# One decoder trunk on one Trainium2 core: transposes of x and single x convolutions stated one behind each weight piece, and the last group's sums stated later

## The chip, the cores and the metric

The kernel runs on one core of one Trainium2 chip. The metric is device time in microseconds (us), one launch; the time before is 1239.31 us, the median of 3 runs (1236.56 to 1241.85). A core has TensorE (PE, matmuls; its weight loads are listed as PEld), VectorE (DVE), ScalarE (ACT), GpSimd (POOL) and SyncE (SP, which here issues DMAs). Each engine works its own queue in order, and waits on semaphores for what others produce.

## The reference, cut to what matters

Two layers over 256 tokens of width 2048. The change lies in layer 0, a Mamba-2 (SSD) mixer with 8 groups of 8 heads:

```python
proj = h @ in_w                                   # z, x, B, C, dt
xBC = silu(conv4(xBC) + b)                        # causal, depthwise, 4 taps
dt = softplus(dt + dt_bias); A = -exp(A_log)
acum = cumsum(dt * A)                             # one chunk of 256 tokens
decay = exp(where(causal, acum_l - acum_s, -inf))
y = einsum("blsgk,bsgkp->blgkp", (C . B) * decay, x * dt)
y = (y + x * D_skip) * silu(z)
yg = y * rsqrt(mean(y ** 2, per group of 512) + eps)
out = (yg * norm_g) @ out_w
```

Layer 1 (dilated attention) and the two layer norms stay as they are.

## The kernel before, in words

All weights are streamed once. A weight arrives in **pieces** of 512 KB (`raw`, 6 buffers, DMAs issued by SP). ACT rounds a piece to `whi` (L100), DVE takes the rest as `wlo = raw - whi` (L102), and PE multiplies with both halves. There are 4 buffers of each half, so the split of a piece waits until PE is done with the piece four before it. A piece of `cm_quad` is 24 matmuls (L151, L152 with `whi`, L153 with `wlo`); a piece of `cm_wide` (L194, L197) is 16 matmuls; a piece of the output product is 12 (L228). In the text the pieces are numbered in the order of their splits from the kernel's start, P70, P151 and so on, with whi#151 and wlo#151 as their halves.

The SSD stage is a loop over groups g. An iteration states, in this order: the product of B and C for the next two groups (odd g only), `scores(g)` (C times B, two matmuls L739, L740), the product of x of group g+1, `stage3` of group g-1, `stage1(g)`, the four convolutions of x of group g+1 (`convolve`), the product of z of group g+1 and `stage2(g)`.

- A convolution `conv` is an ACT scaling (L389), three DVE multiply-adds (L392) and an ACT silu (L394).
- `stage1` takes the decays: relu (L757, 16 times) and exp (L759, twice, and L761, 4 times) on ACT, a DVE product (L762), then 8 transposes of x on PE (L770) with three DVE products out of PSUM (L772 `xd` twice, L777 `xo`), and four ACT copies (L781).
- `stage2`: matmuls L791 and L802, DVE L793, L794, L805, L806, an ACT square (L808). `stage3`: DVE sums L813, L815 and the small matmuls L818, then L820 and a reciprocal root.

Silu and exp/relu lie in different tables of ACT, so that an `ACT_TABLE_LOAD` stands wherever the queue goes from one kind to the other.

The order within each engine is fixed when the program is built: by a scheduler that takes instructions by the place of their statement and their priority (`tc.high_priority()` draws a block forward, `tc.issue_after` puts an instruction behind a named one). `background` states pieces of other work (the adaLN product on DVE, L320) between weight pieces. `latest[-1]` is the last stated split's DVE instruction. After the loop a product runs (`last_scores` at its third piece, q == 2, states stage3 of group 6 and scores and stage1 of group 7), then stage2 of group 7, then `out_pieces`, the output product over the normed groups, to which `y_ahead(q)` is called at each piece; `ylo` (L879) are the low halves of the normed y that it multiplies.

## Time and profile before

| | |
|---|---|
| median of 3 runs | 1239.31 us (1236.56 to 1241.85) |
| the profiled execution, time | 1240.34 us |
| the profiled execution, span | 1238.5 us |
| mean granted TensorE clock | 0.994 |
| SSD stage in the span | about 200 to 533 us |
| HBM read | 332.50 MB, 271 GB/s over the span |

The span is the profiled part of one execution; the time beside it includes what lies around it (1.84 us). Of a row of the timeline, the first number is the start in us from the span's start, the second how long the group on that row was busy, and in brackets stands how long the engine was idle before it and what released it. In a wait table the numbers are total us, times, longest. PEclk is the granted clock of TensorE as a share of full speed.

### The profile page before, as it was taken

The numbers are of one execution on the slowest core, as the hardware profiler recorded it, in microseconds if no ns is written. First come the engines' busy times: TensorE is split into PE (matmuls) and PEld (weight loads), VectorE is DVE, ScalarE is ACT, GpSimd is POOL, SyncE is SP. The second block draws the span as 40 slices with busy tenths as digits, with TensorE's granted clock in tenths as the row PEclk, the third lists the DMA queues.
The fourth block names the chain that finished last, engine by engine and source line by source line (L and its number), as shares of the span: only waits on it lengthen the run. The fifth ranks groups of instructions, "written<-read, shape, count | busy, mean of one in ns | idle before, by whom it ended". The sixth has DMA issues, their size and how long they took to land.

```text
span 1238.5 us, 20144 instructions
## 1 busy us (share of the span) xinstructions
PE 1210.6 (98%) x7772; PEld 1074.9 (87%) x7772; DVE 1026.3 (83%) x1450; ACT 711.5 (57%) x1056; POOL 12.5 (1%) x21
## 2 busy tenths in 40 slices
PE   8999999899999999979999999999999999999998
PEld 8999999888999998868888888888888888888886
DVE  6999987899888999999788678788996885756886
ACT  4555467787698899644344365443444844444751
POOL 0000000000000000000000000000000000000001
PEclk9999999999999999989999999999999999999999
DMA  9999976785767658689898668989997785355563
GB/s 374 421 421 422 422 273 232 250 312 162 217 227 200 153 204 209 145 255 358 324 370 337 244 221 320 352 347 361 373 392 283 276 269 175 115 188 170 189 257 68
DMA packets 81969, 337.06 MB, mean 272 GB/s; under 512 B 9537, under 2 KB 10321, under 8 KB 69073
## 3 DMA queue, kind: packets, MB, share of 16 engines
q1 hardware_dynamic: 80496, 333.59, 75.3%
q0 software_dynamic: 1168, 2.11, 1.0%
q8 instruction: 61, 1.00, 0.3%
q14 instruction: 36, 0.29, 0.1%
q10 hardware_dynamic: 208, 0.08, 0.0%
HBM read 332.50 MB, written 3.24 MB: 271 GB/s over the span
## 4 chain that ended last, share of the span: by engine, by line
PE 73%; DVE 11%; ACT 7%; DMA 6%; issue 3%; SPq 0%; DVEq 0%; ACTq 0%
PE acc L228 23%; PE acc L194 21%; PE acc L197 11%; DMA raw<-in_win 3%; DVE wlo L102 3%; DVE araw L320 3%; PE acc L153 3%; PE acc L151 3%; PE acc L152 3%; ACT whi L100 2%; DVE cacc L392 2%; DMA araw<-in_ada 2%; ACT seg L757 1%; PE py L802 1%; PE acc L238 1%
## 5 line engine op out<-in xcount | busy, mean ns | idle before, releaser
L100 ACT ACTIVATE whi<-raw 128x1024 fp32r<-128x1024 f32 x389 | 408.1, 1057 | 345.0 <-PE acc L194 105.7
L102 DVE TENSOR_TENSOR wlo<-raw,whi 128x1024 fp32r<-128x1024 f32 x389 | 470.2, 1221 | 135.9 <-ACT whi L100 130.5
L194 PE MATMUL acc<-actT,whi 128*128 128x512 f32 x1280 | 401.4, 394 | 0.0
L197 PEld LDWEIGHTS acc<-actT,wlo 128*128 128x128 f32 x1280 | 239.5, 188 | 54.5 <-DVE wlo L102 2.3
L197 PE MATMUL acc<-actT,wlo 128*128 128x256 f32 x1280 | 254.8, 280 | 1.5 <-DVE wlo L102 1.3
L153 PE MATMUL acc<-actT,wlo 128*128 128x256 f32 x884 | 242.1, 279 | 7.9 <-DVE wlo L102 7.9
L151 PE MATMUL acc<-actT,whi 128*128 128x256 f32 x884 | 245.4, 280 | 1.3 <-ACT whi L100 0.7
L152 PE MATMUL acc<-actT,whi 128*128 128x256 f32 x884 | 244.6, 278 | 0.0
L320 DVE SCALAR_TENSOR_TENSOR araw<-araw,cb__72 128x2048 f32<-128x2048 f32 x95 | 217.1, 2285 | 2.0 <-DMA araw<-in_ada 1.7
L194 PEld LDWEIGHTS acc<-actT,whi 128*128 128x128 f32 x1280 | 194.8, 188 | 0.6
L153 PEld LDWEIGHTS acc<-actT,wlo 128*128 128x128 f32 x884 | 164.8, 189 | 10.1 <-DVE wlo L102 9.9
L151 PEld LDWEIGHTS acc<-actT,whi 128*128 128x128 f32 x884 | 166.9, 189 | 2.9 <-ACT whi L100 0.9
L152 PEld LDWEIGHTS acc<-actT,whi 128*128 128x128 f32 x884 | 166.9, 189 | 0.2 <-issue 0.2
L228 PE MATMUL acc<-whi,actT 128*128 128x512 f32 x560 | 144.4, 392 | 0.5 <-ACT whi L100 0.5
L228 PEld LDWEIGHTS acc<-whi,actT 128*128 128x128 f32 x560 | 105.1, 189 | 23.0 <-ACT whi L100 0.9
L228 PE MATMUL acc<-wlo,actT 128*128 128x512 f32 x384 | 104.1, 393 | 0.0
L228 PEld LDWEIGHTS acc<-wlo,actT 128*128 128x128 f32 x384 | 72.7, 189 | 16.0
L228 PE MATMUL acc<-whi,ylo 128*128 128x512 f32 x208 | 57.4, 399 | 1.4 <-DVE ylo L879 1.4
L228 PEld LDWEIGHTS acc<-whi,ylo 128*128 128x128 f32 x208 | 39.7, 191 | 10.1 <-DVE ylo L879 1.5
L757 ACT ACTIVATE seg<-cbc,cumT 128x128 f32<-128x128 f32 x128 | 40.9, 388 | 5.1 <-PE py L802 3.4
L392 DVE SCALAR_TENSOR_TENSOR cacc<-xs,prm,cacc 128x255 f32<-128x255 f32 (+2 forms) x84 | 37.4, 478 | 2.4 <-ACT cacc L389 2.1
L524 ACT ACTIVATE htmp<-xt,mod 128x256 f32<-128x256 f32 x16 | 9.6, 600 | 31.0 <-DVE mod L325 29.3
(331 smaller groups left out, 1092.6 us busy)
## 6 DMA issues: line engine op xcount, KB each, us to landing
araw<-in_ada SPq DMA_DIRECT2D x96, 1024.0 KB, 7.5
raw<-in_win SPq DMA_DIRECT2D x109, 512.0 KB, 9.4
raw<-in_wout SPq DMA_DIRECT2D x64, 512.0 KB, 7.2
raw<-in_wbin SPq DMA_DIRECT2D x64, 512.0 KB, 4.0
raw<-in_wxs SPq DMA_DIRECT2D x48, 512.0 KB, 4.7
raw<-in_wv SPq DMA_DIRECT2D x48, 512.0 KB, 7.2
raw<-in_wk SPq DMA_DIRECT2D x48, 512.0 KB, 7.7
cbc<-cumd SPq DMA_DIRECT2D x16, 512.0 KB, 6.2
```

What stands on the lines that cost most here:

```text
L100: copied.append(S.activation(hi, raw, AF.Copy))
L102: latest.append(V.tensor_tensor(lo, raw, hi.bitcast(F32), op=ALU.subtract))
L151: T.matmul(o, hi[:, k, c_], ahi[:, kt, :], start=first, stop=False, skip_group_check=True)
L152: T.matmul(o, hi[:, k, c_], alo[:, kt, :], start=False, stop=False, skip_group_check=True)
L153: end = T.matmul(o, lo[:, k, c_], ahi[:, kt, :], start=False, stop=kt == k1 - 1, skip_group_check=True)
L194: T.matmul(ps[n], hi[:, k, n * P:n * P + P], both(kt), start=kt == 0, stop=False, skip_group_check=True)
L197: T.matmul(ps[n][:, 0, :], lo[:, k, n * P:n * P + P], high(kt), start=False, stop=kt == KT - 1, skip_group_check=True)
L228: T.matmul(ps[b], a_(kt)[:, b * P:b * P + P], w_[:, k, :], start=a_ is ahi and w_ is hi and kt == k0, stop=w_ is lo and kt == k1 - 1)
L238: end = T.matmul(o, l_, hi[:, k, :], start=False, stop=kt == k1 - 1, skip_group_check=part)
L320: return V.scalar_tensor_tensor(raw, raw, 1.0, cb_, op0=ALU.mult, op1=ALU.mult, accum_out=mod[layer][:, ct, j:j + 1])
L392: V.scalar_tensor_tensor(acc[:, o:], ps[:, :L - o], w[:, j:j + 1], acc[:, o:], op0=ALU.mult, op1=ALU.add)
L757: S.activation(seg[:, hh, b, :], cbc[:, hh, b, :], AF.Relu, bias=cumT[:, b, h0 + hh:h0 + hh + 1], scale=-1.0)
```

## The change

`stage1` is cut in two. What remains makes the decays and the four ACT copies; the new `by_tokens` makes the transposes with `xd` and `xo`, and its DVE instructions are put behind the latest `wlo`. `xs_conv` and `xs_wide` return four single convolutions, each with its DVE part behind the latest `wlo`. These become entries of a list `chores`: first `unit` (stage3 of the group before and `by_tokens`), then the four convolutions; `cm_quad` takes one entry behind a piece from its second on, `cm_wide` likewise. What is left of an older list is emptied ahead of stage1, and `unit` at the latest ahead of stage2. `stage3` of the last group is stated at q == 8 of the first output chunk, without high priority, where it was at q == 1 with it, and the last group's `y_tiles` at q == 6 of the second chunk, where it was at q == 2.

```diff
@@ -174,6 +174,8 @@
                 begin_next()
             end = cm_piece(src, q, ps, ahi, alo, k0=k0, w=w)
             background(*rate)
+            if chores and q > k0 // 2:
+                chores.pop(0)()
         z_end[:] = [end]
         return ps
 
@@ -197,6 +199,8 @@
                     T.matmul(ps[n][:, 0, :], lo[:, k, n * P:n * P + P], high(kt), start=False, stop=kt == KT - 1,
                              skip_group_check=True)
             background(*rate)
+            if chores and q > 0:
+                chores.pop(0)()
         def put():
             for n in range(2):
                 d = dst[:, n, :]
@@ -382,15 +386,16 @@
                      ("bc", 6): (win[3], 12, y[5]), ("z", 6): (win[12], 12, y[6]), ("z", 5): (win[11], 10, y[7])}
             xs, bc, sz = {}, {}, dict(enumerate(szt))
 
-            def conv(ps, ct, dst):
+            def conv(ps, ct, dst, after=None):
 
                 w = pv("convw")[:, 4 * ct:4 * ct + 4]
                 acc = p0.tile([P, L], F32, name="cacc", bufs=3)
                 S.activation(acc, ps, AF.Identity, bias=pv("convb")[:, ct:ct + 1], scale=w[:, 3:4])
                 for j in (2, 1, 0):
                     o = 3 - j
-                    V.scalar_tensor_tensor(acc[:, o:], ps[:, :L - o], w[:, j:j + 1], acc[:, o:],
-                                           op0=ALU.mult, op1=ALU.add)
+                    with tc.issue_after(after) if after is not None else ExitStack():
+                        V.scalar_tensor_tensor(acc[:, o:], ps[:, :L - o], w[:, j:j + 1], acc[:, o:],
+                                               op0=ALU.mult, op1=ALU.add)
                 S.activation(dst, acc, AF.Silu)
 
             def bc_conv(g, t):
@@ -401,8 +406,7 @@
 
             def xs_conv(g, t):
                 xs[g] = xst[g]
-                for i in range(4):
-                    conv(t[i], 4 * g + i, xs[g][:, i, :])
+                return [lambda i=i: conv(t[i], 4 * g + i, xs[g][:, i, :], latest[-1].ins) for i in range(4)]
 
             def hh_(kt):
                 return hhi[:, kt, :]
@@ -414,11 +418,7 @@
                     cm_wide(wxs[2 * g - 4 + w], t[:, 2 * w:2 * w + 2, :], rate=R,
                             moving=(lambda kt: hp[:, :, kt, :], hh_))
 
-                def convolve():
-                    for n in range(4):
-                        conv(t[:, n, :], 4 * g + n, t[:, n, :])
-
-                return convolve
+                return [lambda n=n: conv(t[:, n, :], 4 * g + n, t[:, n, :], latest[-1].ins) for n in range(4)]
 
             def product(kind, g, pre=None):
 
@@ -447,7 +447,7 @@
                                             op=ALU.add)
                     t = [part[:, n, :] for n in range(4)]
                 if kind == "xs":
-                    return lambda: xs_conv(g, t)
+                    return xs_conv(g, t)
                 bc_conv(g, t)
 
             with ExitStack() as c0:
@@ -695,7 +695,8 @@
                 while ended:
                     put_away(*ended.pop())
                 bc_conv(0, tiles(first[0]))
-                xs_conv(0, tiles(first[1]))
+                for convolve in xs_conv(0, tiles(first[1])):
+                    convolve()
             aux = cS.enter_context(tc.tile_pool(name="aux", bufs=2, space=PSUM, reuse_waits="tile"))
             aux2 = cS.enter_context(tc.tile_pool(name="aux2", bufs=2, space=PSUM, reuse_waits="tile"))
             px = pe = cS.enter_context(tc.tile_pool(name="px", bufs=2, reuse_waits="tile"))
@@ -763,25 +764,31 @@
                                     cb[:, 0:2, :].rearrange("p b n -> p (b n)")[:, None, :].to_broadcast([P, 4, L]),
                                     op=ALU.mult)
                     segs.append(seg)
+                for i in range(4):
+                    S.activation(y[g][:, i, :], xs[g][:, i, :], AF.Copy, scale=pv("dsk")[:, 4 * g + i:4 * g + i + 1])
+                return [segs, cb, grow]
+
+            def by_tokens(g, made):
+
+                after = latest[-1].ins
                 xd = px.tile([P, 2, 512], F32, name="xd", bufs=1)
                 for b in range(2):
                     px_ = aux.tile([P, 512], F32, name="aux")
                     for i in range(4):
                         T.transpose(px_[:, i * P:i * P + P], xs[g][:, i, b * P:b * P + P], ident)
                     heads = px_.rearrange("p (h e) -> p h e", h=HPG)
-                    V.tensor_tensor(xd[:, b, :].rearrange("p (h e) -> p h e", h=HPG), heads,
-                                    dtT[:, b, g * HPG:(g + 1) * HPG, None].to_broadcast([P, HPG, 64]),
-                                    op=ALU.mult)
-                    if b == 0:
-                        xo = px.tile([P, 512], F32, name="xo", bufs=1)
-                        V.tensor_tensor(xo.rearrange("p (h e) -> p h e", h=HPG), heads,
-                                        dec[:, g * HPG:(g + 1) * HPG, None].to_broadcast([P, HPG, 64]),
+                    with tc.issue_after(after):
+                        V.tensor_tensor(xd[:, b, :].rearrange("p (h e) -> p h e", h=HPG), heads,
+                                        dtT[:, b, g * HPG:(g + 1) * HPG, None].to_broadcast([P, HPG, 64]),
                                         op=ALU.mult)
-                for i in range(4):
-                    S.activation(y[g][:, i, :], xs[g][:, i, :], AF.Copy, scale=pv("dsk")[:, 4 * g + i:4 * g + i + 1])
-                return segs, xd, cb, xo, grow
-
-            def stage2(g, segs, xd, cb, xo, grow):
+                        if b == 0:
+                            xo = px.tile([P, 512], F32, name="xo", bufs=1)
+                            V.tensor_tensor(xo.rearrange("p (h e) -> p h e", h=HPG), heads,
+                                            dec[:, g * HPG:(g + 1) * HPG, None].to_broadcast([P, HPG, 64]),
+                                            op=ALU.mult)
+                made.extend([xd, xo])
+
+            def stage2(g, segs, cb, grow, xd, xo):
 
                 po = aux.tile([P, 512], F32, name="aux")
                 behind = z_end[-1] if g in (0,2,3,4,7) else None
@@ -840,20 +847,30 @@
                 if g % 2 == 1:
                     product("bc", g + 1)
                 cb = scores(g)
-                convolve = product("xs", g + 1)
-                if rs is not None:
-                    stage3(g - 1, rs)
-                st1 = stage1(g, cb)
-                convolve()
+                convs = product("xs", g + 1)
+                while chores:
+                    chores.pop(0)()
+                made = stage1(g, cb)
+
+                def unit(g=g, made=made, rs=rs):
+                    if rs is not None:
+                        stage3(g - 1, rs)
+                    by_tokens(g, made)
+
+                chores.append(unit)
+                chores.extend(convs)
                 if g < G - 2:
                     product("z", g + 1)
-                rs = stage2(g, *st1)
+                while unit in chores or chores and g == G - 2:
+                    chores.pop(0)()
+                rs = stage2(g, *made)
             st1 = []
 
             def last_scores(q):
                 if q == 2:
                     stage3(G - 2, rs)
                     st1.extend(stage1(G - 1, scores(G - 1)))
+                    by_tokens(G - 1, st1)
 
             def y_scale(g):
 
@@ -907,9 +924,8 @@
         ylo = {g: pn.tile([P, 4, L], F32R, name=f"ylo{g}") for g in (1, 2, 3, 4, 7, 5, 6)}
 
         def y_ahead(q):
-            if q == 1:
-                with tc.high_priority():
-                    stage3(G - 1, rs)
+            if q == 8:
+                stage3(G - 1, rs)
             if q % 2 == 0 and q // 2 + 1 < G - 1:
                 y_tiles(q // 2 + 1)
 
@@ -987,7 +1003,7 @@
                 background(1, 3)
 
         out_pieces(0, 0, KT - 2, y_ahead)
-        out_pieces(1, 0, KT - 2, lambda q: y_tiles(G - 1) if q == 2 else None)
+        out_pieces(1, 0, KT - 2, lambda q: y_tiles(G - 1) if q == 6 else None)
         drain()
         pin[0] = latest[-3].ins
         state[0] = 0
```

The lines of the file move: L389 is L393 after the change, L392 is L397, L394 is L399, L757 to L762 are L758 to L763, L770 is L778, L772 and L777 are L781 and L786, L781 is L768, L791 is L798, L802 is L809, L806 and L808 are L813 and L815, L813 and L815 are L820 and L822, L818 is L825, L228 is L232. No engine but ACT gets more or fewer instructions; on ACT the `ACT_TABLE_LOAD`s go from 32 to 48.

**First place: ACT around the last two groups.** In before the queue of ACT splits P151 to P154 one after the other with little between, and then holds the decays of group 7. Numbers behind a name are buffers (seg_5983 and seg_5998 are the decays of group 7, xs_5582 or xs_5558 the x of group 7, s7_101 its y). This is the part that stands ahead of whi#155, which is the last row:

```order
L761 ACT_TABLE_LOAD
L761 ACTIVATE grow_5980<-cbc_5981 64x256
L759 ACTIVATE seg_5983<-seg_5983 128x1024
L761 ACTIVATE grow_5980<-cbc_5981 64x256
L757 ACTIVATE seg_5998<-cbc_5996,cumT_104 128x128 x5
L808 ACTIVATE sz_5542<-s6_100 128x1024
L757 ACTIVATE seg_5998<-cbc_5996,cumT_104 128x128 x3
L761 ACTIVATE grow_5980<-cbc_5996 64x256
L759 ACTIVATE seg_5998<-seg_5998 128x1024
L761 ACTIVATE grow_5980<-cbc_5996 64x256
L781 ACTIVATE s7_101<-xs_5582,prm_74 128x256 x2
L100 ACTIVATE whi_6092<-raw_6090 128x1024
```

Of the changed program this is what stands between whi#151 and whi#152 (seg_5774 and seg_5789 are the decays of group 6; behind the last row follow an exp L760, an exp L762, four copies L768 and three scalings L393, then whi#152):

```order
L760 ACT_TABLE_LOAD
L760 ACTIVATE seg_5774<-seg_5774 128x1024
L399 ACT_TABLE_LOAD
L399 ACTIVATE xs_5182<-cacc_5711 128x256
L762 ACT_TABLE_LOAD
L762 ACTIVATE grow_5771<-cbc_5772 64x256
L758 ACTIVATE seg_5789<-cbc_5787,cumT_104 128x128 x6
L209 ACTIVATE xs_5558<-acc_5671 128x256
L209 ACTIVATE xs_5558<-acc_5672 128x256
L758 ACTIVATE seg_5789<-cbc_5787,cumT_104 128x128 x2
L762 ACTIVATE grow_5771<-cbc_5787 64x256
```

And this is what follows on whi#152 and three relus, up to the square of group 6 (behind it stand one more table load, two exp L760, three exp L762, eight relus L758 and four copies L768, and then whi#153, whi#154 and whi#155 together):

```order
L399 ACT_TABLE_LOAD
L399 ACTIVATE xs_5558<-cacc_5843 128x256
L399 ACTIVATE xs_5558<-cacc_5849 128x256
L393 ACTIVATE cacc_5861<-xs_5558,prm_74 128x256
L758 ACTIVATE seg_5983<-cbc_5981,cumT_104 128x128
L399 ACTIVATE xs_5558<-cacc_5855 128x256
L758 ACTIVATE seg_5983<-cbc_5981,cumT_104 128x128 x4
L762 ACT_TABLE_LOAD
L762 ACTIVATE grow_5980<-cbc_5981 64x256
L399 ACT_TABLE_LOAD
L399 ACTIVATE xs_5558<-cacc_5861 128x256
L815 ACTIVATE sz_5518<-s6_100 128x1024
```

What stood in one run behind four splits now stands in two runs, one between whi#151 and whi#152 and one between whi#152 and whi#153, and silu and exp change places 7 times in them.

**Second place: PE at the last group's stage2 and the start of the output product.** Of before, from L791 of group 7 (aux<-cb,xo) on; L818 (aux<-cc,sz) is the last group's sum:

```order
L791 MATMUL aux<-cb,xo 128x128 x4
L802 MATMUL py<-seg,xd 64x128 x16
L228 MATMUL acc<-wlo,xs 128x512 x4
L228 MATMUL acc<-whi,xs 128x512 x8
L228 MATMUL acc<-wlo,xs 128x512 x4
L228 MATMUL acc<-whi,actT 128x512 x4
L818 MATMUL aux<-cc,sz 128x1 x2
L228 MATMUL acc<-whi,ylo_6270 128x512 x4
L228 MATMUL acc<-wlo,actT 128x512 x4
```

Of the changed program at the same place:

```order
L798 MATMUL aux<-cb,xo 128x128 x4
L809 MATMUL py<-seg,xd 64x128 x16
L232 MATMUL acc<-whi,xs 128x512 x8
L232 MATMUL acc<-wlo,xs 128x512 x4
L232 MATMUL acc<-whi,xs 128x512 x8
L232 MATMUL acc<-wlo,xs 128x512 x4
L232 MATMUL acc<-whi,actT 128x512 x4
L825 MATMUL aux<-cc,sz 128x1 x2
L232 MATMUL acc<-whi,ylo_6270 128x512 x4
```

One piece part of 8 matmuls went from ahead of the group's L791 to behind its L802, and the small matmuls of the sum still stand behind the first four matmuls of the third output piece. On DVE the queue of before has, between L793 and L815, two splits wlo and four products L871 of other groups, and wlo#162 right ahead of L793; that of the changed program has one split, wlo#162, between L813 and L820, and none of the products.

**Third place: DVE at group 0.** Of before, behind wlo#70, with xd and xo of group 0, cacc of the convolutions of group 1, and wlo#71 on the last row:

```order
L446 TENSOR_TENSOR xs_117<-acc_2517,xs_117 128x512
L772 TENSOR_TENSOR xd_2731<-aux_2732,dtT_102 128x512
L777 TENSOR_TENSOR xo_2738<-aux_2732,dec_105 128x512
L772 TENSOR_TENSOR xd_2731<-aux_2740,dtT_102 128x512
L392 SCALAR_TENSOR_TENSOR cacc_2750<-xs_117,prm_74,cacc_2750 128x255
L392 SCALAR_TENSOR_TENSOR cacc_2756<-xs_117,prm_74,cacc_2756 128x255
L392 SCALAR_TENSOR_TENSOR cacc_2750<-xs_117,prm_74,cacc_2750 128x254
L392 SCALAR_TENSOR_TENSOR cacc_2756<-xs_117,prm_74,cacc_2756 128x254
L392 SCALAR_TENSOR_TENSOR cacc_2750<-xs_117,prm_74,cacc_2750 128x253
L392 SCALAR_TENSOR_TENSOR cacc_2756<-xs_117,prm_74,cacc_2756 128x253
L392 SCALAR_TENSOR_TENSOR cacc_2762<-xs_117,prm_74,cacc_2762 128x255
L102 TENSOR_TENSOR wlo_2833<-raw_2830,whi_2832 128x1024
```

Of the changed program, from the same instruction on, with wlo#71, wlo#72 and wlo#73:

```order
L446 TENSOR_TENSOR xs_117<-acc_2517,xs_117 128x512
L102 TENSOR_TENSOR wlo_2809<-raw_2806,whi_2808 128x1024
L397 SCALAR_TENSOR_TENSOR cacc_2836<-xs_117,prm_74,cacc_2836 128x255
L102 TENSOR_TENSOR wlo_2845<-raw_2842,whi_2844 128x1024
L397 SCALAR_TENSOR_TENSOR cacc_2836<-xs_117,prm_74,cacc_2836 128x254
L397 SCALAR_TENSOR_TENSOR cacc_2872<-xs_117,prm_74,cacc_2872 128x255
L397 SCALAR_TENSOR_TENSOR cacc_2836<-xs_117,prm_74,cacc_2836 128x253
L397 SCALAR_TENSOR_TENSOR cacc_2872<-xs_117,prm_74,cacc_2872 128x254
L102 TENSOR_TENSOR wlo_2881<-raw_2878,whi_2880 128x1024
L781 TENSOR_TENSOR xd_2791<-aux_2792,dtT_102 128x512
L786 TENSOR_TENSOR xo_2798<-aux_2792,dec_105 128x512
L781 TENSOR_TENSOR xd_2791<-aux_2800,dtT_102 128x512
```

wlo#71 stood behind three products and seven multiply-adds, and now stands ahead of them; the same instructions follow one, two or four at a time behind the splits.

More of the change, by code (lines that the diff above doesn't have):

```diff
@@ L105, in trunk @@
     jobs, latest, copied, pin = [], [], [], [None]
-    upcoming, ready, owed = [], [], []
+    upcoming, ready, owed, chores = [], [], [], []
     def settle():
```

## The prediction

> **What bounds the kernel now.** First the page: busy times, the chain, the split lines.
>
> ```profile
> PE 1210.6 (98%) x7772; PEld 1074.9 (87%) x7772; DVE 1026.3 (83%) x1450; ACT 711.5 (57%) x1056; POOL 12.5 (1%) x21
> PE 73%; DVE 11%; ACT 7%; DMA 6%; issue 3%; SPq 0%; DVEq 0%; ACTq 0%
> L100 ACT ACTIVATE whi<-raw 128x1024 fp32r<-128x1024 f32 x389 | 408.1, 1057 | 345.0 <-PE acc L194 105.7
> ```
>
> PE is the bound, so an edit pays only by pauses of PE that it removes or makes. PE's work does not change; I need its pauses in the SSD stage, and what ends them. The waits and PE's timeline show these that end with wlo or with the last group's sums (idle time in the brackets; from one matmul's start to the next a pause costs some 0.17 us more, the pipeline's refill).
>
> ```profile
> 232.24 0.38 PE L153 MATMUL acc<-actT,wlo 128*128 128x256 f32 x1 [3.18 <-DVE wlo L102]
> ...
> 272.01 0.51 PE L197 MATMUL acc<-actT,wlo 128*128 128x256 f32 x2 [1.35 <-DVE wlo L102]
> ...
> 326.56 0.39 PE L153 MATMUL acc<-actT,wlo 128*128 128x256 f32 x1 [1.22 <-DVE wlo L102]
> ...
> 526.31 1.07 PE L228 MATMUL acc<-whi,actT 128*128 128x512 f32 x4
> 532.99 0.98 PE L818 MATMUL aux<-cc,sz 128*128 128x1 f32 x4 [5.61 <-DVE sz L815]
> 535.36 2.07 PE L228 MATMUL acc<-whi,ylo 128*128 128x512 f32 x4 [1.38 <-DVE ylo L879]
> ...
> 540.64 1.18 PE L228 MATMUL acc<-whi,ylo 128*128 128x512 f32 x4
> 541.66 1.09 PE L228 MATMUL acc<-wlo,actT 128*128 128x512 f32 x4
> 542.59 1.07 PE L228 MATMUL acc<-whi,actT 128*128 128x512 f32 x4
> ```
>
> The windows tell which engine is full around each, and that a pause costs clock as well (columns: PE, PEld, DVE, ACT, POOL busy; PEclk; DMA share; GB/s).
>
> ```profile
> 222.00:245.00 23.00, 19.82 (x161) 19.62 (x160) 21.23 (x30) 14.27 (x20) 0.00 (x0) 0.93 0.62 212
> 245.00:288.00 43.00, 41.65 (x311) 38.29 (x311) 41.72 (x57) 33.78 (x59) 0.00 (x0) 1.00 0.84 300
> 422.00:453.00 31.00, 31.00 (x221) 27.98 (x220) 27.63 (x44) 30.76 (x55) 0.00 (x0) 1.00 0.70 216
> 521.00:540.00 19.00, 12.01 (x65) 9.60 (x62) 15.79 (x25) 11.54 (x12) 0.55 (x1) 0.75 0.78 278
> ```
>
> DVE is full at 245 to 288 (41.72 of 43 us), ACT at 422 to 453 (30.76 of 31 us): neither has room there for anything moved in. The clock of 0.93 over 23 us is 1.6 us lost, behind the pause that ends at 232.24, 3.35 us with its refill; at 521 to 540, behind the wait for the sums, it is 0.75 over 19 us.
>
> **Term 1, group 0.** The pause that ends at 232.24 waits for wlo#71, which stood in DVE's queue behind ten other instructions. The order now has it right behind wlo#70, so the pause of 3.4 us and its clock loss of 1.7 us go: -5.1. But nothing leaves DVE, only its order changes, and DVE was nearly full until 270:
>
> ```profile
> 228.21 2.84 DVE L392 SCALAR_TENSOR_TENSOR cacc<-xs,prm,cacc 128x255 f32<-128x255 f32 x7
> 230.97 1.22 DVE L102 TENSOR_TENSOR wlo<-raw,whi 128x1024 fp32r<-128x1024 f32 x1
> ```
>
> PE comes to the next such wait (the row at 272.01, for wlo#83) 5.1 us earlier. DVE gains only about 1.6 us, the little idle time ahead of it (23 - 21.23 us in the window of 222 to 245, less than that behind). So that pause grows from 1.5 to about 5.0 us, +3.5, and is then longer than the 3.35 us that cost clock before: +2.4, between the 1.7 of that case and twice it. Sum **+0.8**. Ends: -1.7 if DVE gains 4 us, all its slack, and no clock is lost; +1.7.
>
> **Term 2, groups 1 to 3.** The pause that ends at 326.56 (1.2 us, 1.4 with its refill) has the same cause in smaller; its split comes a little earlier: **-0.4** (-1.1 to +0.3, from nothing changed to all of it gone with a small new one).
>
> **Term 3, group 4 to 5.** In the full ACT window (422 to 453) the changed order has, between whi#134 and whi#135, three scalings, a silu, a square and one more table load than before, and on DVE, from wlo#133 to wlo#135, 16 multiply-adds (0.41 us each by the row of seven above, 6.5) and stage2's products, two L805 and an L806 (2.5 by the rows under term 5), with nine more of 0.3 to 0.7 us (5) and wlo#134 (1.2): some 15 us. A piece is 2.7 us of PE (12 matmuls of 0.23), and at most four splits are in hand, 11 us. I take 15 less 11 and less the 1.4 us by which DVE is ahead of the third piece's end: **+2.6** (1 if the splits run further ahead, 4.5 if the pause costs clock too).
>
> **Term 4, the last two groups.** Here ACT decides. In before, this is its hole:
>
> ```profile
> 486.65 1.05 ACT L100 ACTIVATE whi<-raw 128x1024 fp32r<-128x1024 f32 x1
> 487.60 0.63 ACT L205 ACTIVATE xs<-acc 128x256 f32<-128x256 f32 x2
> 488.46 1.09 ACT L389 ACTIVATE cacc<-xs,prm 128x256 f32<-128x256 f32 x2 [0.23 <-DVE xs L206]
> 491.77 1.28 ACT L757 ACTIVATE seg<-cbc,cumT 128x128 f32<-128x128 f32 x4 [2.22 <-PE py L802]
> 492.96 0.71 ACT L394 ACTIVATE xs<-cacc 128x256 f32<-128x256 f32 x2
> 493.57 1.26 ACT L757 ACTIVATE seg<-cbc,cumT 128x128 f32<-128x128 f32 x4
> 494.86 1.28 ACT L761 ACT_TABLE_LOAD   x1
> 496.15 0.42 ACT L761 ACTIVATE grow<-cbc 64x256 f32<-64x256 f32 x1
> 496.48 1.04 ACT L759 ACTIVATE seg<-seg 128x1024 f32<-128x1024 f32 x1
> 497.54 0.41 ACT L761 ACTIVATE grow<-cbc 64x256 f32<-64x256 f32 x1
> ...
> 499.45 1.04 ACT L808 ACTIVATE sz<-s 128x1024 f32<-128x1024 f32 x1
> ...
> 503.08 0.91 ACT L781 ACTIVATE s<-xs,prm 128x256 f32<-128x256 f32 x2
> 503.90 3.89 ACT L100 ACTIVATE whi<-raw 128x1024 fp32r<-128x1024 f32 x4
> ```
>
> 16.2 us without a split (from 487.7) cost PE little, since four pieces were split ahead: 0.9 us inside, and behind it three pauses, of which these are the first and the last:
>
> ```profile
> 504.99 0.39 PE L151 MATMUL acc<-actT,whi 128*128 128x256 f32 x1 [0.71 <-ACT whi L100]
> ...
> 509.99 1.19 PE L228 MATMUL acc<-whi,xs 128*128 128x512 f32 x4 [0.61 <-ACT whi L100]
> ```
>
>  From one start to the next I read: relu 0.30 each, silu 0.31, table load 1.29, exp L761 0.38, exp L759 1.06, square 0.95 (its 1.04 less the 0.1 by which such rows overlap), scaling 0.50, copy 0.41, copy L205 0.30, split 0.96. Between whi#151 and whi#152 stand now 3 loads, 2 L759, 1 silu, 3 L761, 8 relus, 2 L205, 4 copies, 3 scalings: 13.6 us. Between whi#152 and whi#153: 4 loads, 16 relus, 4 silus, 1 scaling, 4 L761, 1 square, 2 L759, 4 copies: 17.9 us. whi#151 takes the buffer of P147, so it starts with P147's end. From there to P153's first half: 13.6 + 17.9 + 3 x 0.96 = **34.4 us**. In before that stretch was the time between these rows of PE (the start of P147's last matmuls, and P153's first):
>
> ```profile
> 476.87 0.40 PE L197 MATMUL acc<-actT,wlo 128*128 128x256 f32 x2
> ...
> 497.29 0.36 PE L151 MATMUL acc<-actT,whi 128*128 128x256 f32 x1
> ```
>
> With 0.2 us for those last matmuls it is 20.2 us, nearly all PE work. So +14.2; behind it whi#153 to whi#155 now follow at once, and the three pauses that before's late whi#155 caused go, some 0.6 us each with 0.17 of refill: -2.4; a pause of some 7 us for P153 costs one clock stretch, +1.7. Sum **+13.5**. Ends: 10, if ACT enters the first run a few us ahead of P147's end and no clock is lost; 16, if the silus wait for their DVE multiply-adds.
>
> The trace shows a load at 494.86 straight behind a relu that ends at 494.83, and the exp at 496.15 straight behind the load: 1.28 us and nothing around it. The Trainium skill ("ScalarE: Activation LUTs", section "What ACT_TABLE_LOAD costs") gives about 1283 ns and a drain of about 1380 ns for each switch; the first agrees, the second does not show here, and by it the hole's five more loads would cost 6.9 us more, the sum being that much higher.
>
> **Term 5, the sums of the last group.** Of before, from 526.31 to 540.64 PE has 16 matmuls of the output product and four tiny ones. At the rate behind it (four in 0.93 us) that is 3.7 + 0.4 us; it took 14.3: 10.2 us lost, half to the wait for L815, the rest to ylo and the clock. L815 was late because of the first of these rows of DVE:
>
> ```profile
> 522.72 1.23 DVE L102 TENSOR_TENSOR wlo<-raw,whi 128x1024 fp32r<-128x1024 f32 x1 [2.05 <-ACT whi L100]
> 523.86 0.69 DVE L793 TENSOR_TENSOR xo<-aux,grow 128x512 f32<-128x512 f32 x1
> ...
> 525.86 1.28 DVE L805 TENSOR_TENSOR s<-py,s 128x512 f32<-128x512 f32 x2
> ...
> 527.45 1.22 DVE L806 TENSOR_TENSOR s<-s,sz 128x1024 f32<-128x1024 f32 x1
> ...
> 532.42 0.42 DVE L815 TENSOR_TENSOR sz<-sz 128x256 f32<-128x256 f32 x1
> ```
>
> L793 stood behind it. In the new order it stands ahead, and two splits and four products leave the chain. Walked from the start of L791: L793 and L794 done at 2.2 us, the py products at 3.5, the gating at 4.7, wlo#162 at 5.8, the square beside it, L813 and L815 at 7.8. PE has L791 1.0, L802 1.9 and now 28 output matmuls, 6.4: it comes to L818 at 9.3. No wait; what stays is ylo, about 0.5 to 1 us. **-9.3** (ends -10.2, all of it, and -5, if DVE comes to L793 three or four us late).
>
> **Sum.** 0.8 - 0.4 + 2.6 + 13.5 - 9.3 = **+7.2 us**. From the profiled execution's 1240.34 us (span 1238.5) that is 1247.5; that execution lies 1.0 above the median 1239.31, so against the median I forecast **1246.5 us**. The other 11 of 16 loads added lie in groups 0 to 5, where they are counted in terms 1 to 3 or hidden by ACT's idle time (14.27 of 23 us busy in group 0).
>
> **Rivals.**
> - *The hole costs no more than it did* (faster). If ACT's runs are met by waits that PE has anyway, PE loses about what the hole cost before (0.9 + 2.4), 3 us in place of 13.5: sum -3.3, 1236. For it: 345.0 us idle ahead of splits on the page. Against: 34.4 us of ordered ACT work ahead of P153, and 20.2 us of PE work. It decides below 6.3 us for term 4. Chance 0.12.
> - *The sums still hold PE*. L818 stands in the same place of PE's order, behind four matmuls of the third output piece; if DVE comes late out of the long hole, or the silus in it wait for DVE, the end gives back 4 us and not 9.3: sum +12.5, 1252. For it: DVE 83% busy; against: one split, not three, in its chain. Chance 0.20.
> - *All at the low ends*: terms 1 to 3 at -1.8, the hole at 10, the end at -10: -1.8, 1237.5 to 1241 with one of them less low. It would look as if the change did nothing. Chance 0.14.
> - *A load costs twice what its row shows* where exp and silu change places: five more in the hole at another 1.28 us, +6.4, 1253. The rows at 493.57 to 496.15 speak against it. Chance 0.02.
>
> The clock rows carry a smaller choice. A pause of 3.35 us was followed by 1.6 us of lost clock. The Trainium skill ("TensorE: Matmul & The Clock Gate", section "What's actually happening") has a free-running window of 3413 ns, and half rate after at least one idle window; by that, pauses of 5 us could escape it by chance, and terms 1 and 4 would be 2.4 and 1.7 lower, 1242.4. That pause, a little shorter than such a window, was caught, so I keep the loss.
>
> **How the numbers follow.** Forecast 0.52, its own range 1241 to 1252; the rivals 0.12, 0.20, 0.14, 0.02. The range for 8 in 10 is 1237 to 1254: it leaves out most of the first rival and the far ends. Half a per cent, 6.2 us, is about what a measurement of this kernel can tell from no change. Over 0.5% slower (above 1245.5): 0.32 of the forecast's 0.52, 0.20 and 0.02: 0.54. Faster by over 0.5% (below 1233.1): half of the first rival, 0.06. Within: 0.40.
>
> **What would show it.** Right: no wait of PE at wlo#71 and a longer one at wlo#83; about 34 us between P147's end and P153's start, with two PE pauses of about 7 us there that end with a split; L825 (the old L818) without a wait; ACT_TABLE_LOAD 48 times at 1283 ns. Wrong: PE running through the last two groups, or waiting 5 us at the sum again, or a pause at a place that I hold for even (groups 1 to 3).

## The result, and the profile after

| | before | after |
|---|---|---|
| median | 1239.31 us (1236.56 to 1241.85) | 1260.65 us (1259.26 to 1263.66) |
| profiled execution's span | 1238.5 us | 1258.9 us |
| mean granted TensorE clock | 0.994 | 0.987 |

The ratio is 1.0168, with a 95% interval of 1.0145 to 1.0191: 21 us slower, where 7 us were forecast (1246.5, range 1237 to 1254). From the page of the changed kernel, the busy times and the chain:

```profile
PE 1220.4 (97%) x7772; PEld 1081.8 (86%) x7772; DVE 1026.4 (82%) x1450; ACT 733.0 (58%) x1072; POOL 12.5 (1%) x21
PE 68%; DVE 15%; DMA 8%; ACT 5%; issue 4%; SPq 0%; DVEq 0%; ACTq 0%
```

ACT's busy time grew by 21.5 us, the 16 table loads (16 x 1.283 = 20.5) and little else. That it is as much as the kernel lost is chance: 11 of the added loads lie ahead of P148, where the kernel had lost 1.8 us in all, and 5 in the hole of the last groups. The next table shows where the time went. It gives the start of the same matmul in both timelines; the shift is after less before, and the last column is what the stretch since the row above added:

| place | before, us | after, us | shift | in this stretch |
|---|---|---|---|---|
| groups 0 to 3 done | 425.18 | 425.52 | +0.3 | +0.3 |
| P148 begins | 477.11 | 478.95 | +1.8 | +1.5 |
| the hole is over (94 weight matmuls behind P153's first) | 513.98 | 528.24 | +14.3 | +12.4 |
| first matmul of the last group's stage2 | 519.65 | 539.80 | +20.1 | +5.9 |
| output product, behind the sums | 541.66 | 558.28 | +16.6 | -3.5 |
| output product, late | 690.13 | 710.08 | +19.9 | +3.3 |

Eight matmuls of the output product, about 1.9 us of PE work (four in 0.93 us), lie ahead of the last group's stage2 in before (509.99 us) and behind it in the changed kernel. With the same work in each stretch, the hole cost 14.3 us and the stretch of the sums gave back 5.4.

The waits of the changed kernel in that part (480 to 560 us):

```profile
DVE s L888 <- DMA s<-rootd: 10.6, 1, 10.6
...
PE acc L153 <- DVE wlo L102: 7.3, 3, 3.4
...
PE acc L151 <- ACT whi L100: 5.2, 1, 5.2
```

**The hole.** ACT's timeline from whi#151 to whi#153; P153's first matmul could start only with the last row:

```profile
478.95 1.05 ACT L100 ACTIVATE whi<-raw 128x1024 fp32r<-128x1024 f32 x1
...
493.65 1.04 ACT L100 ACTIVATE whi<-raw 128x1024 fp32r<-128x1024 f32 x1
...
495.59 1.28 ACT L399 ACT_TABLE_LOAD   x1
...
499.88 1.28 ACT L762 ACT_TABLE_LOAD   x1
...
501.61 1.28 ACT L399 ACT_TABLE_LOAD   x1
...
504.29 1.28 ACT L760 ACT_TABLE_LOAD   x1
...
512.85 2.93 ACT L100 ACTIVATE whi<-raw 128x1024 fp32r<-128x1024 f32 x3
```

Windows of the same stretch (columns as before: PE, PEld, DVE, ACT, POOL; PEclk; DMA share; GB/s):

```profile
498.00:516.00 18.00, 7.33 (x35) 6.55 (x35) 15.63 (x37) 17.84 (x34) 1.76 (x3) 0.64 0.30 45
516.00:526.00 10.00, 10.00 (x71) 10.00 (x72) 5.60 (x5) 3.93 (x4) 0.55 (x1) 0.79 0.95 29
526.00:534.00 8.00, 5.58 (x50) 5.38 (x48) 0.73 (x2) 4.46 (x4) 0.00 (x0) 0.99 0.89 357
```

ACT is busy 17.84 of the 18 us from 498 to 516, PE is busy 7.3 of 18 us, and at a clock of 0.64. From whi#151 (478.95) to P153's first matmul (513.94) pass 35.0 us. Table loads stand here between silu and exp alone: no load lies between the silus and the relus L758 behind them at 498.01 and 498.61 us, so relu needed no load of its own here, though the text on the kernel before counts it with exp.

**What was not forecast.** DVE's timeline behind the hole: 10.6 us idle, and then two rows of PE, the pause that this made and the wait for the sums:

```profile
521.44 1.23 DVE L102 TENSOR_TENSOR wlo<-raw,whi 128x1024 fp32r<-128x1024 f32 x1 [1.07 <-ACT whi L100]
533.27 0.48 DVE L888 SCALAR_TENSOR_TENSOR s<-s,prm,s 128x256 f32<-128x256 f32 x1 [10.61 <-DMA s<-rootd]
533.67 1.22 DVE L102 TENSOR_TENSOR wlo<-raw,whi 128x1024 fp32r<-128x1024 f32 x1
```

```profile
534.94 0.58 PE L153 MATMUL acc<-actT,wlo 128*128 128x256 f32 x1 [3.37 <-DVE wlo L102]
...
550.71 0.58 PE L825 MATMUL aux<-cc,sz 128*128 128x1 f32 x4 [0.87 <-DVE sz L822]
```

The wait for the sums itself is nearly gone (0.9 us, before 5.6). But DVE stood at a product L888 of group 2 until the roots of groups 2 to 5 had been read from memory (`s<-rootd`, 512 KB, a broadcast), and the next wlo stood behind it in the queue. DMA queues and issues of the changed kernel from 514.5 to 521 us, and then from 534 to 545 (of a queue: packets, MB, share of the time of the 16 DMA engines; of an issue: count, KB each, median us to landing):

```profile
q1 hardware_dynamic: 37, 0.15, 91.7%
q0 software_dynamic: 32, 0.00, 0.7%
...
raw<-in_wout SPq DMA_DIRECT2D x4, 512.0 KB, 12.5
s<-rootd POOLq DMA_DIRECT2D x1, 512.0 KB, 13.7
rootd<-ay POOLq DMA_DIRECT2D x1, 1.0 KB, 8.9
...
q1 hardware_dynamic: 451, 1.65, 46.7%
...
raw<-in_wout SPq DMA_DIRECT2D x4, 512.0 KB, 3.4
```

Weight pieces of the same size land after 3.4 us where no write of roots is under way and after 12.5 us here. From 516 to 526 us the DMA engines are 95% busy and move 29 GB/s. An estimate from the rows of q1, the weights' queue: a packet took some 2.6 us there (91.7% of 16 engines and 6.5 us, 37 packets) and some 0.18 us later (46.7% of 16 and 11 us, 451). Beside the weights runs `rootd<-ay`, the write of group 6's 256 roots (L828, in before L821): one KB, element by element across partitions, 8.9 us; its own queue q0 has 0.7%. In the changed kernel POOL issues the read 4.6 us behind this write; in before the two DMAs of the roots lie in the other order, and the read lands after 4.6 us. POOL's rows of the changed kernel, then of before:

```profile
514.98 0.72 POOL L828 DMA_DIRECT2D rootd<-ay  x1 [15.43 <-DVE ay L288]
519.53 0.55 POOL L63 DMA_DIRECT2D s<-rootd  x1 [3.84 <-DVE xs L896]
...
510.37 0.55 POOL L63 DMA_DIRECT2D s<-rootd  x1 [15.85 <-DVE at L282]
512.12 0.72 POOL L821 DMA_DIRECT2D rootd<-ay  x1 [1.19 <-DVE ay L284]
```

### The profile page after: what moved, and what is told of

It reads as the page before. It is cut to its first block, busy times and chain, and to the rows that moved or that the text cites. A ratio compares the mean times of both kernels' runs of the same rounds, so it can differ in the third digit from the quotient of the medians.

```text
span 1258.9 us, 20156 instructions
## 1 busy us (share of the span) xinstructions
PE 1220.4 (97%) x7772; PEld 1081.8 (86%) x7772; DVE 1026.4 (82%) x1450; ACT 733.0 (58%) x1072; POOL 12.5 (1%) x21
## 4 chain that ended last, share of the span: by engine, by line
PE 68%; DVE 15%; DMA 8%; ACT 5%; issue 4%; SPq 0%; DVEq 0%; ACTq 0%
PE acc L196 22%; PE acc L232 17%; PE acc L199 11%; DVE araw L324 4%; DVE wlo L102 4%; PE acc L153 3%; PE acc L151 3%; PE acc L152 3%; ACT whi L100 2%; DMA raw<-in_win 2%; DMA raw<-in_wout 2%; DMA araw<-in_ada 2%; DVE cacc L397 1%; DMA s<-rootd 1%; PE acc L242 1%
## 5 line engine op out<-in xcount | busy, mean ns | idle before, releaser
L232 PE MATMUL acc<-whi,actT 128*128 128x512 f32 x560 | 144.5, 393 | 1.1 <-ACT whi L100 1.1
L232 PEld LDWEIGHTS acc<-whi,actT 128*128 128x128 f32 x560 | 105.0, 189 | 23.9 <-ACT whi L100 1.9
L232 PE MATMUL acc<-wlo,actT 128*128 128x512 f32 x384 | 104.0, 393 | 1.6 <-DVE wlo L102 1.6
L232 PEld LDWEIGHTS acc<-wlo,actT 128*128 128x128 f32 x384 | 72.0, 188 | 18.1 <-DVE wlo L102 2.5
L232 PE MATMUL acc<-whi,ylo 128*128 128x512 f32 x208 | 56.9, 396 | 1.6 <-DVE ylo L896 1.6
L232 PEld LDWEIGHTS acc<-whi,ylo 128*128 128x128 f32 x208 | 39.4, 190 | 10.3 <-DVE ylo L896 1.7
L758 ACT ACTIVATE seg<-cbc,cumT 128x128 f32<-128x128 f32 x128 | 40.6, 388 | 2.6 <-DMA cbc<-cumd 2.5
L397 DVE SCALAR_TENSOR_TENSOR cacc<-xs,prm,cacc 128x255 f32<-128x255 f32 (+2 forms) x84 | 38.1, 478 | 0.3 <-ACT cacc L393 0.2
```

The costliest lines, as they stand in the source:

```text
L232: T.matmul(ps[b], a_(kt)[:, b * P:b * P + P], w_[:, k, :], start=a_ is ahi and w_ is hi and kt == k0, stop=w_ is lo and kt == k1 - 1)
L397: V.scalar_tensor_tensor(acc[:, o:], ps[:, :L - o], w[:, j:j + 1], acc[:, o:], op0=ALU.mult, op1=ALU.add)
L758: S.activation(seg[:, hh, b, :], cbc[:, hh, b, :], AF.Relu, bias=cumT[:, b, h0 + hh:h0 + hh + 1], scale=-1.0)
```

## The experiments

**The parts alone.** e1 is before with the late sums only; e2 is the change without them:

```diff
-            if q == 1:
-                with tc.high_priority():
-                    stage3(G - 1, rs)
+            if q == 8:
+                stage3(G - 1, rs)
...
-        out_pieces(1, 0, KT - 2, lambda q: y_tiles(G - 1) if q == 2 else None)
+        out_pieces(1, 0, KT - 2, lambda q: y_tiles(G - 1) if q == 6 else None)
```

> Kernel before with only the late sums (stage3 of the last group at q == 8, its y_tiles at q == 6). Theory: after the wait of 5.6 us for L815 goes, PE loses 1 us or less there, so 8 to 10 us faster: 1229 to 1232. Rival (late sums give back only what the changed kernel showed at that place, 3.5 us, or lose it again to later waits for wlo and whi): 1236 to 1240.

> Changed kernel with the sums of the last group where before had them (q == 1 with high priority, y_tiles at q == 2). Theory: the holes of ACT ahead of P152 and P153 (+13), the pause behind them (+4.7) and the early groups (+1.8) stay, and before's tail comes back: 1259 to 1264. Rival (the late sums cause the pause at 531 and the later ones): 1250 to 1256.

e1: 1240.35 us, ratio 1.000 (0.9978 to 1.0022): the rival. e2: 1262.57 us, ratio 1.0169 (1.0133 to 1.0205): the theory. The late sums gave nothing by themselves. From the waits of e1, 517 to 540 us:

```profile
ACT whi L100 <- DMA raw<-in_wout: 6.7, 1, 6.7
...
PE aux L818 <- DVE sz L815: 6.0, 1, 6.0
```

PE still waits 6.0 us for L815, and ACT 6.7 us for a weight piece: in DVE's queue L793 still stood behind the wlo of that piece. That the chain stood ahead of it in the changed kernel came from the scheduler's whole order there, not from the place of the statement.

**Without table loads.** e3 ends the convolutions with `AF.Identity`, which leaves out the silu.

> Changed kernel in which the convolutions end with Identity in place of Silu (this leaves out the silu of x, B and C), so that 26 of 48 table loads go, 7 of them in the two runs of ACT around whi#152. Theory (the loads are in series with the splits there): 9 us shorter from P147's end to P153's start, and 1246 to 1252 in all. Rival (silu waits for DVE anyway, the loads hide in waits): less than 4 us shorter there, 1256 or more.

It took 1238.85 us (one run). But the scheduler orders by its own costs, and with Identity it put the last groups as in before, with one hole of ACT. So the run doesn't tell what the loads alone cost in the changed order; that stays open. It does show the sums again: its order there is that of before, and PE waits 6.4 us.

**The last groups as before.** e4 states the iterations 5 and 6 in the old order:

```diff
+                if g >= G - 3:
+                    stage3(g - 1, rs)
+                    made = stage1(g, cb, True)
+                    for convolve in convs:
+                        convolve(None)
+                    if g < G - 2:
+                        product("z", g + 1)
+                    rs = stage2(g, *made)
+                    continue
```

> Changed kernel with the iterations g = 5 and 6 stated as before (convolutions together, transposes inside stage1); groups 0 to 4 and the late sums as in the change. Theory: one hole of ACT of 16 us as before, so +13 and the pause behind it (+4.7) go: 1232 to 1240. Rival (the pause at 531 belongs to the late sums, not to the holes): 1241 to 1246.

1247.57 us, ratio 1.0067 (1.0046 to 1.0089): 13 us come back, not the 21 to 28 of the theory, and the time lies above the rival's range too. By the shift against before, the hole costs 1.8 us in place of 12.4 and the pause at 531 is gone, so both belong to the new order of the last groups. What is left of the loss lies ahead of them: at P148 e4 is already 6.6 us behind before, the changed kernel 1.8. Why e4 loses more there stays open.

**Which half makes the hole.** e9 leaves the convolutions together, their DVE part no longer put behind a split, and moves only the transposes; e10 the other way round; e11 is the change with group 7's decays two pieces later:

```diff
-                chores.extend(convs)
+                for convolve in convs:
+                    convolve()
```

```diff
-                if q == 2:
+                if q == 4:
                     stage3(G - 2, rs)
                     st1.extend(stage1(G - 1, scores(G - 1)))
```

> Changed kernel with the four convolutions of x stated together as before; only the transposes (with stage3) go one behind a weight piece, and the sums are late. ACT has 36 table loads, and one run of its own work between whi of the last groups, as before. Theory (the single convolutions cut the splits apart and cost the hole): the 13 us and the pause behind it go, 1237 to 1244. Rival (the transposes make the hole): 1252 or more.

> Changed kernel with the transposes inside stage1 as before; only the convolutions go one behind a weight piece, and the sums are late. ACT has 44 table loads and two runs between the splits of the last groups, now with two splits between them. Theory: most of the hole stays, 1250 to 1262. Rival (it takes the transposes too): 1237 to 1244.

> Changed kernel with the scores and decays of group 7 stated at the fifth piece of the last product in place of the third (q == 4). ACT's second run is then cut in two by whi#154. Theory (PE lacks splits, not work): the pauses between 498 and 515 shrink by 3 to 6 us, 1252 to 1258, if nothing new waits for group 7's decays behind it. Rival (the hole is the bound through stage2 of group 7): 1260 or more.

e9: 1240.64 us, ratio 1.0009 (0.9993 to 1.0025). e10: 1252.68 us, 1.0105 (1.0073 to 1.0137). e11: 1245.67 us, 1.0053 (1.0035 to 1.007), better than its theory had it. By the shift of their profiled runs against before, the hole of 12.4 us is 0.4 in e9, 9.7 in e10 and 5.6 in e11. The single convolutions make most of the hole; the transposes and the late sums together cost nothing. ACT's splits in e11:

```profile
494.68 1.99 ACT L100 ACTIVATE whi<-raw 128x1024 fp32r<-128x1024 f32 x2
499.10 1.04 ACT L100 ACTIVATE whi<-raw 128x1024 fp32r<-128x1024 f32 x1
512.95 1.04 ACT L100 ACTIVATE whi<-raw 128x1024 fp32r<-128x1024 f32 x1
```

Three splits now stand where one stood at 493.65 in the changed kernel, and the wait of PE for whi fell from 5.2 to 1.0 us, with ACT's work the same but two loads. PE lacked splits. That is about 7 of the 15 us that e11 gave back. Another 6 are the pause at 531, which e11 does not have: there the read of the roots goes out 8.0 us ahead of the write of group 6's roots and lands after 5.9 us.

```profile
517.39 0.54 POOL L63 DMA_DIRECT2D s<-rootd  x1 [16.10 <-DVE ay L288]
525.42 0.72 POOL L828 DMA_DIRECT2D rootd<-ay  x1 [7.49 <-DVE ay L288]
```

**The root writes.** e5 (on before) and e6 (on the change) send one packet of 8 bytes a group, so that the values of the group norm are left out; beside the edit shown they write ones to the roots' memory once, ahead of the stage. e7 and e8 turn the roots on PE and send two packets of 512 bytes, with nothing left out; e12 is e9 so.

```diff
-                nc.gpsimd.dma_start(rootd[g * L:g * L + L].rearrange("(b p) -> p b", p=P), rsqrt(ms, "a"))
+                nc.gpsimd.dma_start(rootd[g * L:g * L + 2].rearrange("(b p) -> p b", p=1), rsqrt(ms, "a")[0:1, :])
```

```diff
+                T.transpose(turned, rsqrt(ms, "a"), ident)
+                root = sm.tile([2, P], F32, name="root", bufs=1)
+                V.tensor_copy(root, turned)
+                nc.gpsimd.dma_start(rootd[g * L:g * L + L].rearrange("(b p) -> b p", p=P), root)
```

> Kernel before whose roots go out as one packet of 8 bytes a group in place of 256 packets of 4 bytes (the roots in memory are ones, written once ahead of the stage: this leaves out the group normalisation's values). The order on PE, DVE and ACT is that of before. Theory (weight pieces issued while a root write of 4-byte packets is under way land after 9 to 13 us in place of 5): whi#162 no longer waits for its piece, the wait for the sums falls from 5.8 to under 2 us: 1229 to 1233. Rival (the pieces are late for want of free buffers or rate): unchanged, 1237 to 1241.

> Changed kernel with the same small root packets (the group normalisation's values are left out); order as in the changed kernel. Theory: the read of the roots lands after about 5 us in place of 13.7, DVE waits 10.6 us less for it, the pause of PE at 531 goes, and the later ones in part: 1250 to 1255. Rival (the slow transfers come from the many pieces issued at once behind the hole): 1258 to 1262.

> Kernel before with the roots turned on PE (one transpose) and copied by DVE, and written as two packets of 512 bytes; nothing is left out. Theory: as in e5 less 1 us for the added steps, 1229 to 1234, if the order keeps the sums' chain. Rival: unchanged, 1237 to 1241.

> Changed kernel with the roots turned and written as two packets of 512 bytes. Theory: 1250 to 1256. Rival: 1258 to 1262.

> As e9, with the roots turned on PE and written as two packets of 512 bytes. Theory: the weight pieces behind the root writes land in time, so 3 to 8 us below e9, 1232 to 1238. Rival: no difference to e9.

| run | us | ratio to before (95%) |
|---|---|---|
| e5, before, 8 bytes | 1238.28 | 0.9995 (0.9978 to 1.0011) |
| e7, before, turned | 1239.09 | 1.0002 (0.9986 to 1.0019) |
| e6, change, 8 bytes | 1251.45 | 1.0100 (1.0078 to 1.0121) |
| e8, change, turned | 1251.04 | 1.0103 (1.0073 to 1.0132) |
| e12, e9 turned | 1241.94 | 1.0021 (1.0001 to 1.0042) |

On the change the theory holds: 8 us back by the ratios (1.0168 to 1.0100), with the order on PE, DVE and ACT that of the changed kernel in e6. Its DMA issues, 514.5 to 524 us, and what is left of DVE's wait:

```profile
raw<-in_wout SPq DMA_DIRECT2D x5, 512.0 KB, 4.9
s<-rootd POOLq DMA_DIRECT2D x1, 512.0 KB, 7.2
```

```profile
526.61 0.48 DVE L889 SCALAR_TENSOR_TENSOR s<-s,prm,s 128x256 f32<-128x256 f32 x1 [4.04 <-DMA s<-rootd]
```

The pause of PE at 531 is gone, in e8 too, where the write still has 1 KB: it is the single elements that count, not the bytes. On before the expected 6 to 10 us did not come, nor in e12. In e5 the wait for the sums did fall, to 2.6 us, and 3.1 us of shift came back there; but 2.8 us had been lost in group 0, where a pause of 0.9 us and a lower clock (0.85 from 222 to 245 us, before 0.93) were new. In e7 3.7 us of shift were lost up to the last groups, where its added steps lie, and 4.7 came back at the sums. So on before the slow write costs about 3 to 5 us at the sums, not 10, and the rest of the loss there is the chain itself.

**The chain of the sums once more.** f1 is before with q == 4 in `last_scores`, f2 adds the late sums, f3 is f1 with turned roots.

> Kernel before with the scores and decays of group 7 stated at q == 4 of the last product, nothing else. On DVE the split wlo ahead of L793 and most products of other groups then stand ahead of the chain of the sums, not in it. Theory (the loss at the sums is the place of the chain among splits that wait for late pieces, which the statement of stage3 does not decide): the wait for L815 falls from 5.8 to 3 us or less and the three pauses behind whi#155 go: 1230 to 1235. Rival (the group's own work is then late instead): 1238 or more.

> As f1, with the sums late as in the change. Theory (late sums only move ylo ahead of the root's steps on DVE): within 2 us of f1. Rival (late sums pay once the chain is free of late splits): 3 us or more below f1.

> As f1, with the roots turned on PE and written as two packets of 512 bytes. Theory: 0 to 4 us below f1 at the sums, up to 3 us given back by the added steps in groups 0 to 5: 1229 to 1236. Rival: no better than before, 1237 or more.

f1: 1252.14 us, ratio 1.0112 (1.0093 to 1.0131); f2: 1256.77, 1.0145 (1.0125 to 1.0165); f3: 1243.14, 1.0042 (1.0024 to 1.0059). The theory fell for all three: f1 and f3 lie where their rivals had them, f2 is 4.6 us above f1, which neither side had. For f1 the reason at the sums is the one of the changed kernel, made on before by a single number. POOL's timeline of f1, its DMA issues there (511 to 520 us), and the waits (488 to 545):

```profile
512.27 0.71 POOL L821 DMA_DIRECT2D rootd<-ay  x1 [18.34 <-DVE ay L284]
513.41 0.57 POOL L63 DMA_DIRECT2D s<-rootd  x1 [0.43 <-DVE xs L879]
```

```profile
raw<-in_wout SPq DMA_DIRECT2D x4, 512.0 KB, 12.2
s<-rootd POOLq DMA_DIRECT2D x1, 512.0 KB, 12.8
```

```profile
DVE s L871 <- DMA s<-rootd: 9.7, 1, 9.7
...
PE aux L818 <- DVE sz L815: 9.2, 1, 9.2
```

The read of the roots went out 1.1 us behind the write in place of 1.8 ahead of it, landed after 12.8 us in place of 4.6, and DVE stood 9.7 us with the sums' chain behind it. By the shift, f1 lost 5.2 us in the stretch of the sums and 5.6 in that of the hole, where PE waits 2.9 us for group 6's sums and 3.6 for wlo. In f3, with two packets a write, the read lands after 6.4 us, PE's wait at the sums is 0.4 us, and that stretch gives back 4.4; 3.2 us of the hole stay, and their cause stays open:

```profile
s<-rootd POOLq DMA_DIRECT2D x1, 512.0 KB, 6.4
```

No version ran faster than before beyond the spread of the runs.

## Why the prediction was wrong

- **Terms 1 and 2** (+0.8 and -0.4, together +0.4): +0.3 by the shift. The pause at wlo#71 went, and that at wlo#83 grew (4.0 us idle, before 1.35), as walked. Both parts were smaller than walked, about -3.5 and +4.1 in place of -5.1 and +5.9, so that the close sum is in part luck. The low end of term 1 does not follow from its walk: with 4 us gained by DVE and no clock lost it is -5.1 + 1.1 = -4.0, not -1.7.
- **Term 3** (+2.6): +1.5, within its ends. One pause came there, for wlo at 439.10 us, 0.8 us idle and so smaller than walked.
- **Term 4** (+13.5): +14.3 with the same PE work, +12.4 in the table. The 34.4 us from P147's end to P153 were 35.0 us. Two pauses of 7 us were expected; they came as waits of 1.4 and 0.8 (transposes, for the last silus), 3.3 and 5.2 us, and a lower clock (0.64 over 18 us). Its cause is shown by e9 to e11: the single convolutions, by taking the splits apart, make 9.7 of the 12.4 us by themselves.
- **Term 5** (-9.3): the step that failed. "L793 stood behind it. In the new order it stands ahead" was right, and the wait for L815 fell from 5.6 to 0.9 us. But the walk counted only engine time from L791 on, and took DVE as free at L791. The row that it quoted, 2.05 us of waiting for whi, went back to a late weight piece, and that was not asked about. In the changed kernel the read of the roots held DVE for 10.6 us ahead of L791, and PE lost 5.9 us there, in no term of the sum. DVE came late to the chain as well: from the start of L791 (now L798, 539.80 us) to the end of L815 (now L822, 550.56 us) the walk has 7.8 us, and it took 10.8. With the same PE work the stretch of the sums gave back 5.4 us; it still has waits of 0.9 and, for ylo, 1.6 us, and a clock of 0.84 (548 to 559 us). So +5.9 and -5.4, +0.5 in place of -9.3. Without the single elements of the root write, e6 and e8 give 8 us back.
- **Behind the stage** nothing was forecast and 3.3 us were lost. In e6 2.6 us of these are gone. The last group's root write (578 us) lies beside weights that landed after 13 to 14 us, and PE waited 0.5 us for a whi at 595.61. The larger wait, 1.6 us for wlo at 646.33, stood behind products of DVE that waited 1.2 and 0.9 us for reads of `in_x`; that the root write is its cause is not shown.
- **The rivals**: "the sums still hold PE" had DVE late out of the hole, and 1252; the direction was right, the mechanism (a DMA at the head of DVE's queue) was not named. A load that costs more than its row shows did not appear: 1283 ns each, 48 times. Nor did a long pause escape its loss of clock: behind the pauses that end at 271.21 and 534.94 us it was 0.81 (271.2 to 280) and 0.66 (531 to 540).

## What to carry to other kernels

Count an engine's work between two items that the bound engine needs: as in term 4, that held within a us. But for each instruction at the head of an in-order queue look up its DMA too, and what else is on the DMA queues then, above all small scattered writes. And where a scheduler decides, read the order that it makes: in e1 moving a statement left the chain behind the same split, and in f1 moving one turned round the two DMAs of the roots.

## What the hardware showed that was not expected

A write of 1 KB as 256 single elements of 4 bytes (L821, L828; the profile lists it as 32 packets on POOL's queue) landed after 8.3 to 11.9 us in all runs that have it. The 512 KB weight transfers issued in the 6 us behind one landed after 8.9 to 13.2 us in before and 8.6 to 14.4 in the changed kernel. With one packet of 8 bytes or two of 512 in its place the write itself took 1.5 to 6.2 us (e5 to e8, f3), and the weights in the same 6 us landed after 3.4 to 7.7 (e6) and 3.3 to 9.0 (e8). A broadcast read of 512 KB issued behind such a write landed after 12.8 (f1), 13.9 (f2) and 13.7 us (the changed kernel), but after 8.9 in e10; just ahead of it after 4.5 to 6.4 (before, e1, e4, e9). The Trainium skill ("DMA: Bandwidth & Descriptors", section "Specifications") names 512 bytes as the least for line rate. The slow write of 4-byte elements and the faster one of two packets of 512 bytes agree with it; that large transfers of another queue slow beside such a write is shown by the runs. Why the packets of the whole set of DMA engines slow so (29 GB/s from 516 to 526 us) is not shown by these runs.
